# Attention scores over 64 rows throughout, a head's two maps in the two halves of the rows

## The chip, the core and the metric

The kernel runs on one core of one Trainium2 chip. The metric is the device time of one execution in microseconds; times are told as the median of several runs. Traces come from the hardware profiler, one execution each.

## The reference

One step of a hybrid decoder layer: 1024 prompt tokens and 8 single-token samples go through an input projection, four retention heads, four differential-attention heads, an output projection and a gated MLP. What the change touches is the differential attention over the prompt. Each of its four heads has two query and key maps of 64 features each:

```python
s = jnp.einsum('bqhmd,bkhmd->bhmqk', q, dk).astype(jnp.float32) * (DH_DIFF ** -0.5)
s = s + alibi_bias(qpos, kpos, slopes)[None, :, None]
a = diff_combine(jax.nn.softmax(s, axis=-1), lam)      # p[map 0] - lam * p[map 1]
return jnp.einsum('bhqk,bkhe->bqhe', a.astype(dv.dtype), dv)
```

`m` is the map (0 or 1), `d` runs over 64 features, the mask is causal, queries go in blocks of 128.

## The kernel before

**Precision.** Large products are made from values split in two float32r parts, hi and lo, as three matmuls: hi by hi, hi by lo, lo by hi.

**Phases.** Phase A makes the input projection in 28 blocks of 128 output features by three segments of 344 tokens; one block and segment is a "z unit" of 24 matmuls (lines 112 to 114). The stages of four attention heads (`diff_head`), then of four retention heads, and of the samples' paged attention are generators that are advanced between z units (lines 762 to 775), so that their matmuls stand among those of the projection. From about 570 us on come the output projection's norms, the MLP's two products and the end.

**Order.** The program is written with a framework that sets each engine's order ahead of time: instructions are taken in the order in which they were written, and when the next one's operand or buffer would not be there yet, later ones that are ready are put ahead of it. Each engine then works its list in that order and waits where data is late.

**One attention head.** A head's projected queries and keys lie in `zq` and `zk`, 128 rows by 1024 tokens: map 0 in rows 0 to 63, map 1 in rows 64 to 127. ScalarE and VectorE split them in hi and lo (lines 319 to 322). Then six copies from SBUF to SBUF, issued on SyncE's queue (lines 323 to 328), build doubled tiles for each map m: `qs[m]` holds the map's q_hi in one half of the rows and its q_lo in the other, `ks[m]` holds k_hi in both. So one matmul over 128 rows gives q_hi·k_hi + q_lo·k_hi, and a second one, over the 64 rows of map m, adds q_hi·k_lo (lines 342 and 343).

There are 8 stages per head, one for each block i of 128 queries; a stage has w = 128(i+1) keys. Each map's scores are made in one or two chunks of at most 512 keys, each chunk in a PSUM bank of the tag "S" (three banks). VectorE reads the bank, adds the bias and keeps the running minimum (line 345); ScalarE takes the exponential (397); VectorE combines the maps (406). Two stages later the result is transposed (`tr`) and multiplied with the values (`av_mm`, line 363). In a stage the order is: map 0 whole, map 1's first chunk, `av_mm(i-2)`, map 1's second chunk.

While a head is finished, the next one's copies wait in SyncE's queue together with the loads of weights (line 97) and cache pages (line 459).

Of the kernel before, what the change touches and what calls it, by code (L numbers as in the profile page):

```python
# [9 lines left out]
F32 = mybir.dt.float32  # L10
# [26 lines left out]
# columns of the constant block  # L37
# [14 lines left out]
def step_kernel(ctx: ExitStack, tc: tile.TileContext, gam, g128, xT, w_in, w_o, w_f, w_y, norms, ngb, cst, subln,  # L52
# [37 lines left out]
    # ---------------------------------------------------------------- helpers  # L90
# [26 lines left out]
    def rstd_1(pl, acc):  # L117
        """acc [128, n]: per-partition partial sums of squares -> diagonals of rsqrt(mean + eps), split."""
# [42 lines left out]
    # ================================================================ phase A  # L161
# [6 lines left out]
    # ---- load x, fold in the pre-norm gain, split  # L168
# [60 lines left out]
    # the first two blocks go segment by segment, as x comes in  # L229
# [27 lines left out]
    def tail_a():  # L257
# [6 lines left out]
        # lambda, sub-norm gain  # L264
# [32 lines left out]
    def sub_norm(on, n):  # L297
        """on [128, n, 128] *= rsqrt(mean over the last axis + eps), in place."""
# [9 lines left out]
    # ---- differential attention over the prompt, one head, in stages  # L308
    def diff_head(h):
# [3 lines left out]
        # scores: [q_hi; q_lo] against [k_hi; k_hi], then q_hi against k_lo  # L313
        lo_h, hi_h = slice(0, 64), slice(64, 128)
        ks = [pd.tile([P, 1024], F32R, name=f"ks{m}", tag=f"ks{m}") for m in range(2)]
        qs = [pd.tile([P, 1024], F32R, name=f"qs{m}", tag=f"qs{m}") for m in range(2)]
        kl = pd.tile([P, 1024], F32R, name="kl", tag="kl")
        ql = aux([P, 1024], name="ql", dt=F32R)
        nc.scalar.activation(qs[0], zq[:, 0:T], AF.Copy)
        nc.scalar.activation(ks[0], zk[:, 0:T], AF.Copy)  # L320
        nc.vector.tensor_tensor(ql, zq[:, 0:T], qs[0].bitcast(F32), ALU.subtract)
        nc.vector.tensor_tensor(kl, zk[:, 0:T], ks[0].bitcast(F32), ALU.subtract)
        nc.sync.dma_start(ks[1][lo_h].bitcast(F32), ks[0][hi_h].bitcast(F32))
        nc.sync.dma_start(ks[1][hi_h].bitcast(F32), ks[0][hi_h].bitcast(F32))
        nc.sync.dma_start(qs[1][hi_h].bitcast(F32), qs[0][hi_h].bitcast(F32))
        nc.sync.dma_start(qs[1][lo_h].bitcast(F32), ql[hi_h].bitcast(F32))
        nc.sync.dma_start(ks[0][hi_h].bitcast(F32), ks[0][lo_h].bitcast(F32))
        nc.sync.dma_start(qs[0][hi_h].bitcast(F32), ql[lo_h].bitcast(F32))
# [8 lines left out]
        def score(i, m, n0, w, pt, mn):  # L337
            r = slice(64 * m, 64 * m + 64)
            n1 = min(w, n0 + 512)
            sps = bank("S", "sps")[:, 0:n1 - n0]  # L340
            q = slice(i * P, (i + 1) * P)
            nc.tensor.matmul(sps, lhsT=qs[m][:, q], rhs=ks[m][:, n0:n1], start=True, stop=False)
            nc.tensor.matmul(sps, lhsT=qs[m][r, q], rhs=kl[r, n0:n1], start=False, stop=True)  # L343
            mo = pa.tile([P, 1], F32, tag="mn", bufs=6, name="mn")
            nc.vector.tensor_tensor_reduce(pt[:, n0:n1], sps, bias[:, 1024 - w + n0:1024 - w + n1],
                                           -1.0, mn, ALU.add, ALU.min, mo)
            return mo
# [32 lines left out]
        for i in range(8):  # L380
# [6 lines left out]
            pm_ = []  # L387
            for m in range(2):
                pt = aux([P, 1024], name="pt")
                mn = score(i, m, 0, w, pt, 3e38)  # L390
                if m == 1 and i > 1:
                    av_mm(i - 2)
                    if i == 5:
                        on0 = post1(0)
                if w > 512:
                    mn = score(i, m, 512, w, pt, mn)
                nc.scalar.activation(pt[:, 0:w], pt[:, 0:w], AF.Exp, bias=mn, scale=-1.0,
                                     accum_out=sm[:, m:m + 1])
                pm_.append(pt)
# [28 lines left out]
    # ---- paged differential attention of the samples, in stages of a page  # L428
    def sample_attention():
        ptt = pk.tile([1, NS * NPAGE], I32, name="ptt")  # L430
        nc.sync.dma_start(ptt, ptab)
        # queries as rows, one sample's row on every partition
# [101 lines left out]
        # weights with the keys on partitions: [key, page, sample, head]  # L534
# [64 lines left out]
    # ---- retention, one head, in stages  # L599
    def ret_head(h):  # L600
# [15 lines left out]
        # natural values and keys, and the decayed queries, take the places of the transposed ones  # L616
# [22 lines left out]
        # samples: the state's part, sample b in row 32 * (b % 4) + b // 4  # L639
# [11 lines left out]
        # the new key's part  # L651
# [6 lines left out]
        # new keys and values as rows, in three groups of 32: hi, lo, hi against hi, hi, lo  # L658
# [59 lines left out]
    # ---- the rest of the input projection, with the heads' stages woven in  # L718
# [70 lines left out]
    # what is left of the sides, beside the first output blocks' products with the finished heads  # L789
# [27 lines left out]
    split_last(2)  # L817
    closed(LATE["pk"], PR["cm"], LATE["pb"], pa_cm)

    # ================================================================ phase W: output projection, both norms  # L820
    wo_cm, wo = opened("wo")
    ft_cm, ft = opened("ft", "right")
    pw_cm, pw = opened("pw", "right")
# [429 lines left out]
```

## Time and profile before

| what | value |
|---|---|
| median of 3 runs | 1430.91 us |
| the runs | 1428.03, 1430.91, 1433.99 us |
| span of the profiled execution | 1426.5 us |
| TensorE matmul busy (PE) | 1382.5 us, 97% |
| VectorE busy (DVE) | 814.3 us, 57% |
| ScalarE busy (ACT) | 512.1 us, 36% |
| GpSimd busy (POOL) | 321.8 us, 23% |
| mean granted TensorE clock | 0.989 |

The profiled execution has no time on record beside its span; the median of the runs lies 4.4 us above the span, for what lies around the first and the last instruction. PE's matmuls are pipelined, so their durations overlap, and what one costs is read from start to start.

### The profile page before, as it was taken

How to read it: one execution, taken by the hardware profiler on the slowest of the kernel's cores; microseconds unless marked ns; L12 is line 12 of the kernel's file. 1: busy time of each engine (PE TensorE's matmuls, PEld its weight loads, DVE VectorE, ACT ScalarE, POOL GpSimd, SP SyncE). 2: the span in 40 equal slices, each digit the busy share in tenths (PEclk: the TensorE clock that was granted, in tenths of full speed). 3: DMA queues.
4: the chain of work that ended last, by engine and by line, in shares of the span. 5: the costliest groups of instructions: out<-in, count | busy, mean ns of one | idle time of the engine just before them, and what ended most of it. 6: DMA issues, size and time to landing. Idle time of an engine off the chain costs nothing.

```text
span 1426.5 us, 22325 instructions
## 1 busy us (share of the span) xinstructions
PE 1382.5 (97%) x8475; PEld 1315.5 (92%) x8475; DVE 814.3 (57%) x1656; ACT 512.1 (36%) x1016; POOL 321.8 (23%) x289
## 2 busy tenths in 40 slices
PE   6999989999999999999999999999999999989998
PEld 6979788888999999999999999999999999989976
DVE  7664677887589866477533323333232445575585
ACT  6243433426221225344322222222221235445544
POOL 4200084754355621332000000000000000050140
PEclk9999999999999999999999999999999999999999
DMA  5414166673355534132111101011110144344363
GB/s 214 120 48 118 41 191 198 218 212 118 132 175 177 165 129 150 60 140 110 68 52 37 60 31 60 33 57 45 45 60 30 60 169 145 121 156 141 119 201 124
DMA packets 67148, 161.59 MB, mean 113 GB/s; under 512 B 8283, under 2 KB 20699, under 8 KB 66659
## 3 DMA queue, kind: packets, MB, share of 16 engines
q1 hardware_dynamic: 60322, 148.57, 31.7%
q10 hardware_dynamic: 6720, 11.62, 2.2%
q8 instruction: 66, 1.08, 0.3%
q14 instruction: 40, 0.32, 0.1%
HBM read 134.93 MB, written 18.94 MB: 108 GB/s over the span
## 4 chain that ended last, share of the span: by engine, by line
PE 78%; DVE 9%; POOL 4%; issue 3%; DMA 3%; ACT 1%; SPq 0%; POOLq 0%; DVEq 0%; ACTq 0%
PE gp L112 6%; PE gp L113 6%; PE gp L114 6%; PE up L114 6%; PE up L113 6%; PE up L112 6%; PE ps_in L112 5%; PE ps_in L114 5%; PE ps_in L113 5%; PE ps_y L1063 4%; PE ps_y L1064 4%; PE ps_y L1062 4%; PE sps L343 2%; DVE acc_v L583 2%; PE ops L363 2%
## 5 line engine op out<-in xcount | busy, mean ns | idle before, releaser
L112 PE MATMUL ps_in<-xh,wh 128*128 128x344 f32 x672 | 227.0, 338 | 6.8 <-ACT xh L191 5.8
L113 PE MATMUL ps_in<-xl,wh 128*128 128x344 f32 x672 | 220.6, 328 | 2.3 <-DVE xl L192 2.3
L114 PE MATMUL ps_in<-xh,wl 128*128 128x344 f32 x672 | 221.2, 329 | 1.1 <-DVE wl L107 1.1
L112 PE MATMUL gp<-hh,wh 128*128 128x346 f32 x528 | 170.3, 322 | 0.0
L113 PE MATMUL gp<-hl,wh 128*128 128x346 f32 x528 | 170.0, 322 | 0.0
L114 PE MATMUL gp<-hh,wl 128*128 128x346 f32 x528 | 169.4, 321 | 0.0
L114 PE MATMUL up<-hh,wl 128*128 128x344 f32 x528 | 169.3, 321 | 0.0
L113 PE MATMUL up<-hl,wh 128*128 128x344 f32 x528 | 169.1, 320 | 0.0
L112 PE MATMUL up<-hh,wh 128*128 128x344 f32 x528 | 169.0, 320 | 0.0
L107 DVE TENSOR_TENSOR wl<-wraw,wh 128x1024 fp32r<-128x1024 f32 (+1 forms) x81 | 102.1, 1262 | 95.2 <-ACT wh L106 92.8
L106 ACT ACTIVATE wh<-wraw 128x1024 fp32r<-128x1024 f32 (+1 forms) x81 | 84.6, 1045 | 184.3 <-PE gp L113 92.0
L112 PEld LDWEIGHTS ps_in<-xh,wh 128*128 128x128 f32 x672 | 130.7, 194 | 12.8 <-ACT xh L191 5.8
L113 PEld LDWEIGHTS ps_in<-xl,wh 128*128 128x128 f32 x672 | 130.9, 195 | 4.1 <-DVE xl L192 3.7
L1013 DVE TENSOR_TENSOR wyl<-wyraw,wyh 128x1024 fp32r<-128x1024 f32 x66 | 83.5, 1265 | 87.8 <-ACT wyh L1012 86.5
L114 PEld LDWEIGHTS ps_in<-xh,wl 128*128 128x128 f32 x672 | 130.6, 194 | 2.0 <-DVE wl L107 1.4
L1062 PE MATMUL ps_y<-ah,wyh 128*128 128x388 f32 x352 | 120.4, 343 | 3.1 <-ACT wyh L1012 3.1
L1064 PE MATMUL ps_y<-ah,wyl 128*128 128x388 f32 x352 | 120.6, 343 | 0.2 <-DVE wyl L1013 0.2
L1063 PE MATMUL ps_y<-al,wyh 128*128 128x388 f32 x352 | 120.4, 342 | 0.4 <-DVE al L1024 0.4
L927 DVE SCALAR_TENSOR_TENSOR c<-gp,cwt,c 128x344 f32<-128x344 f32 (+1 forms) x66 | 37.7, 570 | 131.2 <-ACT c L925 131.2
L159 POOL TENSOR_TENSOR acc<-acc,sq 128x344 f32<-128x344 f32 (+1 forms) x56 | 58.4, 1043 | 226.4 <-ACT sq L158 160.6
L954 POOL COPY sct<-sct 128x176 f32<-128x176 f32 x1 | 0.5, 516 | 463.5 <-DVE sc L949 463.5
L925 ACT ACTIVATE c<-gp,cbt,cwt 128x344 f32<-128x344 f32 (+1 forms) x66 | 41.7, 632 | 175.3 <-PE gp L114 175.3
(251 smaller groups left out, 3008.5 us busy)
## 6 DMA issues: line engine op xcount, KB each, us to landing
wyraw<-in_w_y SPq DMA_DIRECT2D x66, 512.0 KB, 3.3
wraw<-in_w_f SPq DMA_DIRECT2D x44, 512.0 KB, 3.2
pg<-in_kpool SPq DMA_DIRECT2D x64, 256.0 KB, 3.1
pg<-in_vpool SPq DMA_DIRECT2D x64, 256.0 KB, 3.0
wraw<-in_w_in SPq DMA_DIRECT2D x27, 512.0 KB, 4.0
x<-in_xT SPq DMA_DIRECT2D x3, 1376.0 KB, 5.7
x1d<-x ACTq DMA_DIRECT2D x3, 1376.0 KB, 5.7
wraw<-in_w_o SPq DMA_DIRECT2D x8, 512.0 KB, 3.2
```

Source lines behind the costliest of these rows:

```text
L106: nc.scalar.activation(hi[:, k], raw[:, k], AF.Copy)
L107: nc.vector.tensor_tensor(lo[:, k], raw[:, k], hi[:, k].bitcast(F32), ALU.subtract)
L112: nc.tensor.matmul(ps, lhsT=wh[:, k, :], rhs=ah[:, k, n0:n1], start=(first and i == 0), stop=False)
L113: nc.tensor.matmul(ps, lhsT=wh[:, k, :], rhs=al[:, k, n0:n1], start=False, stop=False)
L114: nc.tensor.matmul(ps, lhsT=wl[:, k, :], rhs=ah[:, k, n0:n1], start=False, stop=(last and i == len(order) - 1))
L159: eng.tensor_tensor(acc, acc, sq, ALU.add)
L925: nc.scalar.activation(c[:, 0:n], gp[:, 2:2 + n], AF.Identity, bias=cbt[:, j:j + 1], scale=cwt[:, j, 2:3])
L927: nc.vector.scalar_tensor_tensor(c[:, 0:n], gp[:, 1:1 + n], cwt[:, j, 1:2], c[:, 0:n], ALU.mult, ALU.add)
L1013: nc.vector.tensor_tensor(wl, raw, wh.bitcast(F32), ALU.subtract)
L1062: nc.tensor.matmul(pss[d], lhsT=wh[:, i, w], rhs=ah, start=(f == 0), stop=False)
L1063: nc.tensor.matmul(pss[d], lhsT=wh[:, i, w], rhs=al, start=False, stop=False)
L1064: nc.tensor.matmul(pss[d], lhsT=wl[:, i, w], rhs=ah, start=False, stop=(f == NF - 1))
```

## The change

The doubled tiles and the six copies per head go. The four split tiles `qh`, `ql`, `kh`, `kl` keep both maps side by side in the two halves of the rows. `score` now makes both maps' chunk in one call: it takes two banks, and issues six matmuls over 64 rows, the two maps in turn (rows 0 to 63, then 64 to 127) for each of the three products. A stage's order is: both maps' first chunk, `av_mm(i-2)`, both maps' second chunk, then both exponentials. `ql` moves from the shared "aux" buffers to the pool `pd`. Elsewhere only comments are dropped.

```diff
-        ks = [pd.tile([P, 1024], F32R, name=f"ks{m}", tag=f"ks{m}") for m in range(2)]
-        qs = [pd.tile([P, 1024], F32R, name=f"qs{m}", tag=f"qs{m}") for m in range(2)]
-        kl = pd.tile([P, 1024], F32R, name="kl", tag="kl")
-        ql = aux([P, 1024], name="ql", dt=F32R)
-        nc.scalar.activation(qs[0], zq[:, 0:T], AF.Copy)
-        nc.scalar.activation(ks[0], zk[:, 0:T], AF.Copy)
-        nc.vector.tensor_tensor(ql, zq[:, 0:T], qs[0].bitcast(F32), ALU.subtract)
-        nc.vector.tensor_tensor(kl, zk[:, 0:T], ks[0].bitcast(F32), ALU.subtract)
-        nc.sync.dma_start(ks[1][lo_h].bitcast(F32), ks[0][hi_h].bitcast(F32))
-        nc.sync.dma_start(ks[1][hi_h].bitcast(F32), ks[0][hi_h].bitcast(F32))
-        nc.sync.dma_start(qs[1][hi_h].bitcast(F32), qs[0][hi_h].bitcast(F32))
-        nc.sync.dma_start(qs[1][lo_h].bitcast(F32), ql[hi_h].bitcast(F32))
-        nc.sync.dma_start(ks[0][hi_h].bitcast(F32), ks[0][lo_h].bitcast(F32))
-        nc.sync.dma_start(qs[0][hi_h].bitcast(F32), ql[lo_h].bitcast(F32))
+        kh, kl, qh, ql = (pd.tile([P, 1024], F32R, name=n, tag=n) for n in ("kh", "kl", "qh", "ql"))
+        nc.scalar.activation(qh, zq[:, 0:T], AF.Copy)
+        nc.scalar.activation(kh, zk[:, 0:T], AF.Copy)
+        nc.vector.tensor_tensor(ql, zq[:, 0:T], qh.bitcast(F32), ALU.subtract)
+        nc.vector.tensor_tensor(kl, zk[:, 0:T], kh.bitcast(F32), ALU.subtract)
...
-        def score(i, m, n0, w, pt, mn):
-            r = slice(64 * m, 64 * m + 64)
+        def score(i, n0, w, pts, mns):
             n1 = min(w, n0 + 512)
-            sps = bank("S", "sps")[:, 0:n1 - n0]
+            sps = [bank("S", "sps")[:, 0:n1 - n0] for _ in range(2)]
             q = slice(i * P, (i + 1) * P)
-            nc.tensor.matmul(sps, lhsT=qs[m][:, q], rhs=ks[m][:, n0:n1], start=True, stop=False)
-            nc.tensor.matmul(sps, lhsT=qs[m][r, q], rhs=kl[r, n0:n1], start=False, stop=True)
-            mo = pa.tile([P, 1], F32, tag="mn", bufs=6, name="mn")
-            nc.vector.tensor_tensor_reduce(pt[:, n0:n1], sps, bias[:, 1024 - w + n0:1024 - w + n1],
-                                           -1.0, mn, ALU.add, ALU.min, mo)
-            return mo
+            for j, (a, b) in enumerate(((qh, kh), (ql, kh), (qh, kl))):
+                for m in range(2):
+                    r = slice(64 * m, 64 * m + 64)
+                    nc.tensor.matmul(sps[m], lhsT=a[r, q], rhs=b[r, n0:n1], start=(j == 0), stop=(j == 2))
+            out = []
+            for m in range(2):
+                mo = pa.tile([P, 1], F32, tag="mn", bufs=6, name="mn")
+                nc.vector.tensor_tensor_reduce(pts[m][:, n0:n1], sps[m], bias[:, 1024 - w + n0:1024 - w + n1],
+                                               -1.0, mns[m], ALU.add, ALU.min, mo)
+                out.append(mo)
+            return out
...
-            pm_ = []
+            pm_ = [aux([P, 1024], name="pt") for _ in range(2)]
+            mns = score(i, 0, w, pm_, (3e38, 3e38))
+            if i > 1:
+                av_mm(i - 2)
+                if i == 5:
+                    on0 = post1(0)
+            if w > 512:
+                mns = score(i, 512, w, pm_, mns)
             for m in range(2):
-                pt = aux([P, 1024], name="pt")
-                mn = score(i, m, 0, w, pt, 3e38)
-                if m == 1 and i > 1:
-                    av_mm(i - 2)
-                    if i == 5:
-                        on0 = post1(0)
-                if w > 512:
-                    mn = score(i, m, 512, w, pt, mn)
-                nc.scalar.activation(pt[:, 0:w], pt[:, 0:w], AF.Exp, bias=mn, scale=-1.0,
+                nc.scalar.activation(pm_[m][:, 0:w], pm_[m][:, 0:w], AF.Exp, bias=mns[m], scale=-1.0,
                                      accum_out=sm[:, m:m + 1])
-                pm_.append(pt)
```

## Rows read from the trace of the kernel before

**Rows 1.** The page: its span, and busy time of the engines in all.

```profile
span 1426.5 us, 22325 instructions
...
PE 1382.5 (97%) x8475; PEld 1315.5 (92%) x8475; DVE 814.3 (57%) x1656; ACT 512.1 (36%) x1016; POOL 321.8 (23%) x289
```

**Rows 2.** Stretches: busy us (instructions) of PE, PEld, DVE, ACT, POOL; clock; DMA.

```profile
60.00:180.00 120.00, 119.92 (x679) 100.38 (x677) 67.24 (x191) 51.92 (x123) 5.01 (x10) 0.99 0.29 85
180.00:375.00 195.00, 186.53 (x1115) 164.34 (x1115) 156.19 (x341) 76.78 (x171) 118.97 (x95) 0.98 0.60 184
220.00:240.00 20.00, 19.99 (x95) 16.09 (x96) 15.84 (x48) 8.24 (x23) 12.80 (x11) 0.91 0.62 199
340.00:360.00 20.00, 19.56 (x110) 15.68 (x109) 20.00 (x45) 8.14 (x14) 14.12 (x12) 1.00 0.55 171
```

**Rows 3.** Line 342: count, min/median/max ns, first and last start, counts by shape.

```profile
L342 PE MATMUL sps<-ks,qs x96: 219/444/512, 75.2 to 356.1; 128*128 128x512 f32 x48, 128*128 128x128 f32 x16, 128*128 128x256 f32 x16, 128*128 128x384 f32 x16
```

**Rows 4.** PE in order of time, 112.8 to 115.4 us: start, duration, line.

```profile
112.78 1.60 PE L363 MATMUL ops<-z,pt 128*128 128x128 f32 x12
114.14 0.47 PE L342 MATMUL sps<-ks,qs 128*128 128x512 f32 x1
114.54 0.49 PE L343 MATMUL sps<-kl,qs 64*128 64x512 f32 x1
114.97 0.42 PE L112 MATMUL ps_in<-xh,wh 128*128 128x344 f32 x1
115.23 0.32 PE L113 MATMUL ps_in<-xl,wh 128*128 128x344 f32 x1
115.39 0.32 PE L114 MATMUL ps_in<-xh,wl 128*128 128x344 f32 x1
```

**Rows 5.** Weight loads (PEld) of the same stretch; in brackets idle time before.

```profile
114.54 0.18 PEld L343 LDWEIGHTS sps<-kl,qs 64*128 64x128 f32 x1 [0.24 <-issue]
114.96 0.19 PEld L112 LDWEIGHTS ps_in<-xh,wh 128*128 128x128 f32 x1 [0.24 <-issue]
115.07 0.19 PEld L113 LDWEIGHTS ps_in<-xl,wh 128*128 128x128 f32 x1
```

**Rows 6.** PE in order of time, 75.9 to 78.2 us, head 0's first scores.

```profile
75.91 0.32 PE L343 MATMUL sps<-kl,qs 64*128 64x128 f32 x1
76.16 0.38 PE L342 MATMUL sps<-ks,qs 128*128 128x256 f32 x1
76.48 0.38 PE L343 MATMUL sps<-kl,qs 64*128 64x256 f32 x1
76.79 0.38 PE L342 MATMUL sps<-ks,qs 128*128 128x256 f32 x1
...
77.41 0.45 PE L342 MATMUL sps<-ks,qs 128*128 128x384 f32 x1
77.78 0.44 PE L343 MATMUL sps<-kl,qs 64*128 64x384 f32 x1
78.15 0.46 PE L114 MATMUL ps_in<-xh,wl 128*128 128x344 f32 x1
```

**Rows 7.** PE in order of time at 1353 us, all matmuls of 128 rows.

```profile
1352.77 0.39 PE L1102 MATMUL ps_n<-wyh,ah 128*128 128x512 f32 x1
1353.00 0.39 PE L1103 MATMUL ps_n<-wyl,ah 128*128 128x512 f32 x1
```

**Rows 8.** PE in order of time at 430.6 us, 128 rows by 32 columns.

```profile
430.63 0.66 PE L558 MATMUL os_ps<-acc_v,ez 128*32 128x128 f32 x16
431.22 0.43 PE L112 MATMUL ps_in<-xh,wh 128*128 128x344 f32 x1
```

**Rows 9.** Instructions on the score banks: VectorE's pass over them.

```profile
L345 DVE CUSTOM_DVE_ANT_0 pt<-sps,bias x64: 280/682/693, 75.8 to 357.3; 128x512 f32<-128x512 f32 x40, 128x128 f32<-128x128 f32 x8, 128x256 f32<-128x256 f32 x8, 128x384 f32<-128x384 f32 x8
```

**Rows 10.** The chain that ended last, in order of time: start, us, what.

```profile
216.55 3.32 DMA ks<-ks
```

**Rows 11.** Waits from 60 to 380 us: waiter, releaser, total us, times, longest.

```profile
PE sps L342 <- DMA ks<-ks: 0.7, 1, 0.7
```

More of the change, by code (lines that the diff above doesn't have):

```diff
@@ L312, in diff_head @@
         nc.sync.dma_start(bias, alibi[h])
-        lo_h, hi_h = slice(0, 64), slice(64, 128)
-        ks = [pd.tile([P, 1024], F32R, name=f"ks{m}", tag=f"ks{m}") for m in range(2)]
-        qs = [pd.tile([P, 1024], F32R, name=f"qs{m}", tag=f"qs{m}") for m in range(2)]
-        kl = pd.tile([P, 1024], F32R, name="kl", tag="kl")
-        ql = aux([P, 1024], name="ql", dt=F32R)
-        nc.scalar.activation(qs[0], zq[:, 0:T], AF.Copy)
-        nc.scalar.activation(ks[0], zk[:, 0:T], AF.Copy)
-        nc.vector.tensor_tensor(ql, zq[:, 0:T], qs[0].bitcast(F32), ALU.subtract)
-        nc.vector.tensor_tensor(kl, zk[:, 0:T], ks[0].bitcast(F32), ALU.subtract)
-        nc.sync.dma_start(ks[1][lo_h].bitcast(F32), ks[0][hi_h].bitcast(F32))
-        nc.sync.dma_start(ks[1][hi_h].bitcast(F32), ks[0][hi_h].bitcast(F32))
-        nc.sync.dma_start(qs[1][hi_h].bitcast(F32), qs[0][hi_h].bitcast(F32))
-        nc.sync.dma_start(qs[1][lo_h].bitcast(F32), ql[hi_h].bitcast(F32))
-        nc.sync.dma_start(ks[0][hi_h].bitcast(F32), ks[0][lo_h].bitcast(F32))
-        nc.sync.dma_start(qs[0][hi_h].bitcast(F32), ql[lo_h].bitcast(F32))
+        kh, kl, qh, ql = (pd.tile([P, 1024], F32R, name=n, tag=n) for n in ("kh", "kl", "qh", "ql"))
[3 more added lines that the diff above has]
+        nc.vector.tensor_tensor(kl, zk[:, 0:T], kh.bitcast(F32), ALU.subtract)
         vn = zv[:, 0:T].rearrange("p (a b) -> p a b", b=P)
```

## The prediction

> **What bounds the kernel now.** I read the page first: TensorE is busy nearly all of the 1426.5 us span, no other engine above 57% [rows 1]. The stretches come next, since the change touches only the attention heads. Heads 0 and 1 lie between 60 and 180 us: PE has next to no idle time there, VectorE is busy 56%. Heads 2 and 3 lie between 180 and 375 us, where the samples' cache pages run too: PE idles 8.5 us of 195, VectorE is busy 80% in the mean and all of 340 to 360 us [rows 2]. So a microsecond of TensorE time saved in heads 0 and 1 should reach the end; in heads 2 and 3 VectorE stands close behind.
>
> Then the order of time on PE, because durations overlap and hide what a matmul costs. Between matmuls of 128 rows, start to start is 0.16 us for 344 columns [rows 4] and 0.23 for 512 [rows 7]: columns at 2.4 GHz, the upper level (granted clock near 1.00 [rows 2]), plus about 0.02. Around the 64-row matmul of line 343 this breaks: from line 342 to 343 0.40 us for 512 columns, from 343 to the next matmul 0.43, and from that one 0.26 where 0.16 is usual [rows 4]. The weight loads say why: at the change of 128 to 64 rows, and back, the load stands idle 0.24 us, starts only when the matmul before is through, and can't run ahead, while the second load after the change again follows at 0.11 us [rows 5]. So going into 64 rows costs 0.40 - 0.23 = 0.17 us and coming out 0.43 - 0.23 = 0.20, 0.37 in all; the further 0.10 behind it is taken as equal before and after.
>
> The Trainium skill, "TensorEngine Tiling (Array Packing)", Key Properties, says that changing the tiling mode drains the engine, and that changing only the tile doesn't. The trace agrees with the first half (0.37 us a round trip, rows 4 and 5); no row shows the second.
>
> **The scores before.** Line 342 has 96 matmuls: 48 of 512 columns, 16 each of 128, 256 and 384 [rows 3]; line 343 has as many. That is 24 pairs of maps with 512 columns and 8 each of the other widths. Start to start a map's two matmuls cost 0.40 + 0.43 at 512 columns [rows 4], 0.37 + 0.37 at 384, 0.32 + 0.31 at 256, and 0.25 twice at 128 (from line 343's row) [rows 6]. A pair of maps thus costs 1.66, 1.48, 1.26, 1.00 us, in all 24 x 1.66 + 8 x 3.74 = 69.8 us.
>
> **The scores after.** A pair becomes six 64-row matmuls in one block: one way in and out (0.37 us) in place of two. What the six cost is not shown before, since no two 64-row matmuls are neighbours there. Three bounds:
> - *Halves overlap, free weight loads*: three steps of 0.23, 0.18, 0.13, 0.07 us (columns plus 0.02), with 0.37: 1.06, 0.91, 0.76, 0.58. Change: 24 x -0.60 + 8 x (-0.57 - 0.50 - 0.42) = -26.3 us.
> - *Halves overlap, but loads go one by one* at the 0.11 us spacing [rows 5]: a step is at least 0.22: 1.06, then 1.03 for all others. Change: -14.4 + 8 x (-0.45 - 0.23 + 0.03) = -19.6 us.
> - *Halves one after the other*: six times 0.23, 0.18, 0.13, 0.11, with 0.37: 1.75, 1.45, 1.15, 1.03. Change: 24 x 0.09 + 8 x (-0.03 - 0.11 + 0.03) = +1.3 us. The half more columns eat what the saved changes give.
>
> Nearest to this are 16 matmuls of 128 columns over four groups of 32 array columns, 0.59 us from their first start to the next shape's [rows 8]; one by one they would be 16 x 0.07 = 1.1 us at least. So parts of the array do work at once here, by columns; by rows is my inference. I take the middle one, -19.6.
>
> The Trainium skill, "TensorE: Matmul & The Clock Gate", Part 3, says that matmuls in different row groups run at once; by it alone the sum would be the first bound's. Its section on LDWEIGHTS says that load time goes with columns and not rows, which the rows bear out (0.18 against 0.19 us, rows 5), and that is the second's.
>
> **Order and banks.** A pair needs two of three banks, so a second pair waits for VectorE's pass over the first pair's map 0, 0.69 us at 512 columns [rows 9], which now begins only near the block's end. In a stage of i >= 4 the cover is `av_mm`, 6 to 12 instructions of 0.11 us (12 in 1.36 [rows 4]), 0.7 to 1.3 us: just enough. Where stages follow each other without a z unit, only a few transposes cover it. Where a bank is late, map 0's three matmuls go ahead of map 1's and nothing overlaps. I take 12 of 48 pairs so: they gain nothing, and -19.6 becomes -14.7.
>
> **VectorE behind it.** Its instructions are the same in number and size. Heads 2 and 3 hold half of the saving, 7 us; with VectorE at 80% to 100% I take half of that as lost in waits: -14.7 + 3.5 = -11.2. Lost to nothing or wholly, that is -14.7 or -7.4.
>
> **The copies.** 24 issues go from SyncE's queue, six per head, and with them the time from split to first score. PE stood waiting for a copy once, 0.7 us [rows 11], at head 2's start, where a copy of 3.32 us is on the chain that ended last [rows 10]; behind it the clock was at its lower level for part of 220 to 240 us: mean 0.91, 0.09 x 20 = 1.8 us lost [rows 2]. Loads of weights and pages (lines 97, 459) queued behind these copies; they come sooner. Elsewhere z units hide the copies. Together 0 to -2.5; I take -2. `ql`'s move and the later exponentials I cost at nothing: two stages lie between the exponential and the transposes; if that cover fails PE would wait about one more exponential.
>
> **Sum:** -11.2 - 2 = -13 us on the span, 1413.5 us; with the 4.4 us that the median lies above the span, **1418 us**, -0.9%.
>
> **The rivals.**
> - *The halves don't overlap, or VectorE takes the gain back.* For: no row shows two halves at work together, and VectorE is full in 340 to 360 us [rows 2]. Against: columns overlap [rows 8], and heads 0 and 1 have slack. Time: +1.3 - 2, 1430 us, no change. The Trainium skill, "TensorEngine Tiling (Array Packing)", PSUM Bottleneck, warns of this: faster tiles don't empty the banks faster.
> - *The blocks break up.* When a bank or a transpose comes mid-block, 128-row matmuls get in and each map is an excursion of three again: per map 3 steps + 0.37 = 1.06, 0.91, 0.76, 0.70 against 0.83, 0.74, 0.63, 0.50, in all 48 x 0.23 + 16 x (0.17 + 0.13 + 0.20) = +19 us; with the copies 1448 us. Against: in the shown stretches line 342 and 343 stand together, with nothing of lines 112 to 114 between a map's two [rows 4, 6].
> - *Each change of half drains like a change of mode* (slower). Every one of the six then costs like line 343: 6 x 0.43, 0.37, 0.32, 0.25 + 0.17 = 2.75, 2.39, 2.09, 1.67, in all 24 x 1.09 + 8 x (0.91 + 0.83 + 0.67) = +45 us: 1474 us. It decides for slower by 0.5% from about 0.033 us per change on: (7.2 + 2 - 1.3) / (48 x 5).
>
> **How the numbers follow.** What a measurement of this kernel can tell from no change is about 0.5%, 7.2 us. Forecast 0.55 (0.51 faster, 0.04 same); no overlap or gain taken back 0.26 (0.03, 0.21, 0.02); broken blocks 0.11 (0, 0.02, 0.09); drains 0.08 (slower). Faster 0.54, same 0.27, slower 0.19. The range reaches from the first bound's full gain with the copies, 1430.9 - 28.3 = 1403, to 1440, past the second case and to the lower part of broken blocks; left out are the drains, most of broken blocks and a little below. The forecast's own range is 1403 to 1424.
>
> **What would show it.** Right: rows 0 to 63 and 64 to 127 starting within hundredths of a us of each other; steps of about 0.23 us per two 512-column matmuls; 48 blocks, not 96, each with one idle load in and one out; PE's time on scores near 50 us; the gain there already at 180 us, with more waits on VectorE behind it; no wait on copies. Wrong: a start 0.23 us behind its neighbour's (no overlap), 0.43 (drains), or lines 112 to 114 within a block (broken up). A clock at its lower level in the blocks would also upset the sum.

## The result, and the profile after

The changed kernel took **1437.57 us** in the median (1432.11 to 1442.05, 13 runs), the kernel before 1428.44 us (1425.71 to 1434.11, 13 runs) on the same chip: ratio 1.0055, 95% interval [1.0039, 1.0071]. It is slower by 0.55%, 9 us at the medians, where 13 us of gain were forecast.

The page of the changed kernel, span and busy times, answers to [rows 1]:

```profile
span 1432.6 us, 22455 instructions
...
PE 1369.0 (96%) x8571; PEld 1311.9 (92%) x8571; DVE 816.6 (57%) x1656; ACT 509.8 (36%) x1016; POOL 321.7 (22%) x289
```

TensorE is busy 13.5 us less, with 96 matmuls more, while the span is 6.1 us longer: the work went down and the idle time went up. The order of time on PE shows what became of a pair of maps, first at 512 columns, then at 128 (columns: start, duration, engine, line, tile, shapes, count; two instructions in one row start within hundredths of a us of each other):

```profile
78.69 0.38 PE L291 MATMUL tp<-ct,pt 128*128 128x128 f32 x2
79.01 0.51 PE L334 MATMUL sps<-kh,qh 64*128 64x512 f32 x2
79.34 0.40 PE L334 MATMUL sps<-kh,ql 64*128 64x512 f32 x2
79.58 0.41 PE L334 MATMUL sps<-kl,qh 64*128 64x512 f32 x2
79.91 0.71 PE L357 MATMUL ops<-z,pt 128*128 128x128 f32 x4
...
86.44 0.33 PE L334 MATMUL sps<-kh,qh 64*128 64x128 f32 x2
86.60 0.28 PE L334 MATMUL sps<-kh,ql 64*128 64x128 f32 x2
86.71 0.27 PE L334 MATMUL sps<-kl,qh 64*128 64x128 f32 x2
86.92 0.66 PE L291 MATMUL tp<-ct,pt 128*128 128x128 f32 x4
```

The halves do work at once: 0.24 us from the second two matmuls to the third two at 512 columns, and 0.11 us at 128 columns, where the one-by-one loads of the middle bound would have made it 0.22. The weight loads of the two halves start together as well:

```profile
79.01 0.19 PEld L334 LDWEIGHTS sps<-kh,qh 64*128 64x128 f32 x2 [0.17 <-issue]
79.11 0.19 PEld L334 LDWEIGHTS sps<-kh,ql 64*128 64x128 f32 x2
79.35 0.20 PEld L334 LDWEIGHTS sps<-kl,qh 64*128 64x128 f32 x2
```

A 512-column pair takes 0.90 us from its first start to the next instruction's, not the 1.66 of before.

The stretches answer to [rows 2] (from, to, length; busy us and count of PE, PEld, DVE, ACT, POOL; clock; DMA share; GB/s):

```profile
60.00:180.00 120.00, 117.69 (x784) 103.61 (x783) 73.68 (x206) 54.45 (x129) 13.84 (x16) 1.00 0.20 67
180.00:375.00 195.00, 170.68 (x1056) 153.77 (x1056) 149.48 (x324) 70.23 (x156) 109.16 (x88) 0.93 0.51 159
```

Between 180 and 375 us TensorE stands idle 24.3 us instead of 8.5, and its mean granted clock is 0.93 instead of 0.98 (1.00 is the upper of its two levels, 2.4 GHz). What it waited for there (total, times, longest):

```profile
PE sps L334 <- DVE mn L338: 10.1, 6, 4.1
PE tp L291 <- DVE pt L398: 8.9, 3, 4.2
PE tp L291 <- DVE z L219: 3.8, 2, 3.4
```

These waits, 22.8 us of the 24.9 that the view lists, are behind VectorE: score passes, combines, evacuations of z units. The wait for a copy [rows 11] is gone.

**Where the time went.** Progress is measured by z units: 24 matmuls of lines 112 to 114 each, counted in order of time from the start, so that unit n is the same work in both kernels. "Before" and "changed" are us from the start of one unit to the start of the other; idle is PE's within them. The two profiled executions lie 6.1 us apart, the medians 9.1; the table divides the former.

| z units | holds | before (idle) | changed (idle) |
|---|---|---|---|
| to 27 | heads 0 and 1 | 197.1 | 189.7 |
| 27 to 57 | heads 2 and 3, cache pages | 197.9 (7.1) | 211.4 (21.8) |
| of these 30 to 36 | head 2's core | 48.4 | 61.1 |
| of these 48 to 54 | head 3's core | 40.3 | 47.1 |
| 57 to 87 | retention heads | 164.8 (2.7) | 165.8 (3.4) |

Start to start, score matmuls cost 69.2 us before (34.5 + 34.7 for the two pairs of heads) and 44.5 after (20.7 + 23.7). The instructions beside them, transposes and `av_mm`, became dearer by 11 us in all; part of the way into and out of the 64-row blocks is now read there. Heads 0 and 1 bring 7.4 us, units 27 to 30 another 4.7 (3.2 of it idle time); head 2's core loses 12.7 and head 3's 6.8.

**Head 2's loss.** The chain of work that ended last, cut to 180 to 280 us, has this share by line in the changed kernel:

```profile
by line: DMA pg<-in_kpool 21.1%; DVE sc L473 11.7%; DVE pt L398 9.8%; POOL pg L482 9.6%; issue 7.3%; DVE wl L107 4.9%; DVE pt L338 4.9%; PE ps_in L114 4.0%; DVE z L219 3.7%; PE ps_in L112 3.5%; PE ps_in L113 3.4%; DMA wraw<-in_w_in 3.2%; DV
```

42.4% of it is the samples' key pages: load, GpSimd's product (482), VectorE's sum (473), which frees the buffer for the next load. The z units' matmuls have 10.9%. One turn of it, just behind unit 36 (start, duration, what), then VectorE and PE in order of time at the same place:

```profile
263.44 5.81 DMA pg<-in_kpool
...
269.38 1.30 POOL pg L482
...
270.71 0.69 DVE sc L473
...
272.98 2.28 DVE pt L398
```

```profile
270.71 0.69 DVE L473 TENSOR_REDUCE sc<-pg 128x8 f32<-128x512 f32 x1 [2.90 <-POOL pg L482]
271.31 0.14 DVE L395 COPY r<-rs 128x1 f32<-128x1 f32 x1
271.37 0.55 DVE L397 SCALAR_TENSOR_TENSOR cf<-sm,nlam,rs 128x1 f32<-128x1 f32 x1
271.84 1.21 DVE L317 TENSOR_TENSOR ql<-z,qh 128x1024 fp32r<-128x1024 f32 x1
272.98 2.28 DVE L398 SCALAR_TENSOR_TENSOR pt<-pt,cf 128x1024 f32<-128x1024 f32 x1
```

```profile
270.87 0.31 PE L114 MATMUL ps_in<-xh,wl 128*128 128x344 f32 x1
275.41 0.87 PE L291 MATMUL tp<-ct,pt 128*128 128x128 f32 x3 [4.22 <-DVE pt L398]
```

VectorE works its list in order. The sum's place comes, the page's product isn't there, VectorE stands 2.90 us; the combine behind it, which the transposes need, comes that much later, and PE stands 4.22 us. The split `ql` of the next head (1.21 us) stands between the two as well.

VectorE has more to do in head 2's core than before. Units 30 to 36 of the kernel before, then of the changed one:

```profile
214.90:263.30 48.40, 47.69 (x251) 38.85 (x249) 39.63 (x100) 20.25 (x50) 27.59 (x24) 0.96 0.63 206
202.70:263.90 61.20, 51.74 (x297) 43.72 (x295) 55.04 (x119) 19.77 (x51) 45.14 (x36) 0.89 0.63 189
```

It is busy 55.0 us of 61.2 where it was busy 39.6 of 48.4: 30 key sums (20.2 us) fall there in place of 17 (11.3 us), and its instructions take 9.8 us longer, in all, than the same ones in the kernels without page arithmetic (experiment 3), where it was 5.1. Since a longer stretch also takes in more page work, this alone doesn't say which came first.

### The profile page after: what moved, and what is told of

Same layout as the page of the kernel before. It is cut to its first block, busy times and chain, and to the rows that moved or that the text cites. A ratio compares the mean times of both kernels' runs of the same rounds, so it can differ in the third digit from the quotient of the medians.

```text
span 1432.6 us, 22455 instructions
## 1 busy us (share of the span) xinstructions
PE 1369.0 (96%) x8571; PEld 1311.9 (92%) x8571; DVE 816.6 (57%) x1656; ACT 509.8 (36%) x1016; POOL 321.7 (22%) x289
## 4 chain that ended last, share of the span: by engine, by line
PE 64%; DVE 11%; DMA 4%; POOL 4%; issue 3%; ACT 2%; SPq 0%; POOLq 0%; DVEq 0%; ACTq 0%
PE gp L112 6%; PE gp L113 6%; PE up L114 6%; PE gp L114 6%; PE up L113 6%; PE up L112 6%; PE ps_y L1055 3%; PE ps_y L1056 3%; PE ps_y L1054 3%; PE ps_in L112 3%; PE ps_in L114 3%; PE ps_in L113 3%; DVE acc_v L575 2%; POOL pg L482 2%; DMA pg<-in_kpool 1%
```

## The experiments

Ratios are to the kernel before on the same chip. Letters in the expectations: theory A blames the changed order within a stage, B the pages' load on VectorE in heads 2 and 3, C the missing copies, P the places of the page sums in VectorE's list, D the meeting of a faster TensorE with VectorE and GpSimd where the pages run.

**1. The order alone.** The tiles, copies and matmuls of before, in the changed order of a stage:

```diff
+            for m in range(2):
+                nc.tensor.matmul(sps[m], lhsT=qs[m][:, q], rhs=ks[m][:, n0:n1], start=True, stop=False)
+                nc.tensor.matmul(sps[m], lhsT=qs[m][r, q], rhs=kl[r, n0:n1], start=False, stop=True)
```

> The kernel before with its doubled tiles and its 128-row matmuls, but in the changed order: a call makes both maps' chunk in two banks, both exponentials come last. PE's work on scores is as before (69.8 us). Theory A (the pair in two of three banks, and the later exponentials, make TensorE stand wherever VectorE is late): slower by 8 to 20 us, with 10 us or more of waits of the scores on line mn between 60 and 380 us (before: 1.3). Theory B (the order does no harm; a shorter score stage alone meets VectorE's load from the cache pages in heads 2 and 3): within 5 us of before, waits on mn under 4 us.

1431.43 us, ratio 1.0007 [0.9991, 1.0023]. The scores' waits on `mn`, matmuls' and weight loads' together as in the expectations, are 6.4 us (1.3 before), between the two theories. The order does no harm by itself that shows in the time: A alone falls.

**2. One map at a time.** 64-row matmuls without copies, in the old order, each map's three in a row:

```diff
             for j, (a, b) in enumerate(((qh, kh), (ql, kh), (qh, kl))):
-                for m in range(2):
-                    r = slice(64 * m, 64 * m + 64)
-                    nc.tensor.matmul(sps[m], lhsT=a[r, q], rhs=b[r, n0:n1], start=(j == 0), stop=(j == 2))
+                nc.tensor.matmul(sps, lhsT=a[r, q], rhs=b[r, n0:n1], start=(j == 0), stop=(j == 2))
```

> The changed kernel's tiles and 64-row matmuls without copies, but one map after the other, in the order and with the one bank per call of the kernel before, so that the halves never work together. From the sum, each map is then three steps and 0.37 us: +19 us of TensorE time, -2 for the copies. Theory A: waits on mn back near before (under 4 us), 1440 to 1450 us in all, and the time lost lies evenly over the four heads. Theory B: the same time, since TensorE is no faster than before and VectorE never in the way.

1443.93 us, 1.0087 [1.0061, 1.0114]. The time lies where it was expected, but not for the reason given. The scores cost 49.6 us, 5 more than interleaved and 20 fewer than before, because the maps overlap without being written in turns (71 score matmuls start within 0.05 us of the one before, 114 in the changed kernel):

```profile
242.50 0.39 PE L333 MATMUL sps<-kl,qh 64*128 64x512 f32 x1
242.51 0.50 PE L333 MATMUL sps<-kh,qh 64*128 64x512 f32 x2
```

Map 0's third product and map 1's first start 0.01 us apart. Whether the framework's order or the engine brought them together wasn't looked into. The loss isn't spread over the four heads either: unit 27 starts 7.5 us sooner than in the kernel before, units 27 to 57 take 19.9 us longer, and the scores' waits on `mn` are 34 us, not under 4. So with cheap scores in the old order the kernel is slow too: the loss goes with the cheap scores and not with the pairing.

**3. No page arithmetic.** GpSimd's products and VectorE's sums of all key pages, and the products and sums of the value pages but the first of each sample, are left out, in both kernels; the loads stay in the program.

```diff
-                nc.gpsimd.tensor_tensor(kp, kp, qb.rearrange("p (a b) -> p a b", b=P), ALU.mult)
-                if held:
-                    reduce_page(*held)
-                held = (kp, b, p)
...
+                    if p:
+                        pass
```

> The changed kernel without the arithmetic on the samples' cache pages (the products and sums of the key pages, and all but the first value pages; the loads stay): VectorE and GpSimd are relieved in heads 2 and 3 alone. To be read beside the kernel before with the same work left out. Theory A: the bank waits stay in part, as the order is the same in all heads, and heads 0 and 1 have few: changed minus before between -12 and 0 us. Theory B: the whole saving of TensorE time reaches the end, changed minus before -18 to -25 us.

> The kernel before without the arithmetic on the samples' cache pages, as in the run beside it. Both theories: 5 to 15 us faster than before, since its idle time of some 8 us between 180 and 300 us goes.

Changed 1393.76 us, 0.9738 [0.9704, 0.9772]; before 1414.75 us, 0.9888 [0.9853, 0.9922]. Without the pages' arithmetic the change is worth 21.0 us. In units 9 to 27 TensorE's time for scores, transposes and `av_mm` together falls by 9.7 us, in 27 to 57 by 9.8. With the arithmetic the kernel before takes 14 us longer and the changed one 44.

The loads stay, but not in their place. With no product that holds a buffer, the last of the 64 key loads is issued at 133 us in the changed kernel and at 166 in the one before (with the arithmetic at 288 and 312). So these runs, and those of experiment 4 without key products, take the key pages' loads out of heads 2 and 3 together with the arithmetic.

**4. Parts of the pages.** The key half alone left out, then VectorE's key sums alone (`reduce_page`) with GpSimd's products kept, each in both kernels.

```diff
-                if held:
-                    reduce_page(*held)
                 held = (kp, b, p)
```

> The changed kernel with the key pages' arithmetic left out (GpSimd's product and VectorE's sum of each of the 64 key pages; their loads and the value pages' work stay). Without any page arithmetic the change was worth -21.0 us, with all of it +8.3. Theory 'each half at its head' (key pages cost head 2 its gain, value pages cost head 3 its): against the before kernel with the same omission the change is worth about half, -10 to -15 us, and z units 30 to 36 take about 48 us as before. Rival 'key pages alone': -20 us or so. Rival 'value pages alone': 0 to +8 us.

> The kernel before with the same work left out: the other side of the comparison. The whole page arithmetic cost it 14 us; about half of that here, 1420 to 1424 us.

> The changed kernel with VectorE's sums of the key pages left out, GpSimd's products kept. Theory 'VectorE's list is too full': this is worth nearly all that leaving out the whole key half is worth. Rival 'GpSimd at work stretches VectorE's instructions': with the products still running the combines (line 398's) stay near 2 us instead of 1.15, and at most half of it comes back.

> The kernel before with the same sums left out: the other side of the comparison. By either theory within 3 us of the kernel before without the whole key half.

| left out | before | changed | change is worth | PE idle, units 27 to 57, before / changed |
|---|---|---|---|---|
| nothing | 1428.44 | 1437.57 | +9.1 | 7.1 / 21.8 |
| key sums | 1425.07 | 1429.63 | +4.6 | 5.1 / 21.0 |
| key sums and products | 1416.67 | 1407.93 | -8.7 | 1.2 / 6.5 |
| all page arithmetic | 1414.75 | 1393.76 | -21.0 | 1.1 / 0.5 |

Each half costs its part: key pages 17.8 us of the swing, value pages 12.3. Of the key half, the sums are the smaller part, 4.5 us, of medians whose intervals are 2 to 3 us wide to each side. As the whole cause "VectorE's list is too full" doesn't hold: the changed kernel without sums is 8 us faster, but in the traces it gains 5.3 us before unit 27, and in units 27 to 57 TensorE idles as before. The other 13.3 us go when the products go too, and with them the loads that they hold back into these heads. The stretch from 180 to 280 us in the changed kernel without sums, then without the key half:

```profile
180.00:280.00 100.00, 86.51 (x514) 77.15 (x514) 63.66 (x114) 31.42 (x79) 80.83 (x63) 0.90 0.66 213
180.00:280.00 100.00, 99.77 (x660) 91.40 (x661) 49.88 (x138) 37.75 (x93) 6.07 (x9) 1.00 0.22 77
```

VectorE is busy 63.7 us in the first and TensorE still stands; in the second GpSimd is nearly idle, the DMA's 213 GB/s are 77, and TensorE hardly stands. Two expectations were missed: -8.7 us is less than the -10 to -15 of "each half at its head", and the kernel before without sums is 8.4 us slower than without the key half, not within 3; products and loads cost it too.

With products and without sums, POOL, DVE and PE in order of time:

```profile
181.54 8.75 POOL L482 TENSOR_TENSOR pg<-pg,qb 128x512 f32<-128x512 f32 x7
190.22 1.02 POOL L305 TENSOR_TENSOR rrn<-ss,ct 128x4 f32<-128x4 f32 x1
```

```profile
191.28 1.74 DVE L306 TENSOR_TENSOR on<-on,rrn 128x512 f32<-128x512 f32 x1 [7.17 <-POOL rrn L305]
...
211.27 0.86 DVE L397 SCALAR_TENSOR_TENSOR cf<-sm,nlam,rs 128x1 f32<-128x1 f32 x1
212.17 1.34 DVE L398 SCALAR_TENSOR_TENSOR pt<-pt,cf 128x128 f32<-128x128 f32 x1
```

```profile
193.17 1.09 PE L291 MATMUL tp<-ct,on 128*128 128x128 f32 x4 [4.80 <-DVE on L306]
```

and the same VectorE instructions in the changed kernel without the key half:

```profile
184.60 0.69 DVE L306 TENSOR_TENSOR on<-on,rrn 128x512 f32<-128x512 f32 x1 [1.18 <-POOL rrn L305]
...
203.13 0.21 DVE L397 SCALAR_TENSOR_TENSOR cf<-sm,nlam,rs 128x1 f32<-128x1 f32 x1
203.37 0.35 DVE L398 SCALAR_TENSOR_TENSOR pt<-pt,cf 128x128 f32<-128x128 f32 x1
```

Two ways show in this kernel. A small power on GpSimd (`rrn`, 1.02 us) stands behind a run of products, VectorE waits 7.17 us for it instead of 1.18, and PE 4.80 behind that. And beside running products VectorE's `on`, `cf` and combine take 1.74, 0.86 and 1.34 us instead of 0.69, 0.21 and 0.35. How much of the idle time is the one and how much the other wasn't separated.

In the full changed kernel the first way is small: between 170 and 380 us VectorE waits for `rrn` 2.8 us in all, 1.1 at the longest, and no wait of TensorE is put down to `on`. There VectorE's waits for GpSimd are those for key products, 15.4 us, and they were 13.1 in the kernel before. The second way is no larger over the whole of heads 2 and 3: measured against the kernels without page arithmetic, VectorE's instructions of units 27 to 57 are 15.9 us longer in the changed kernel and 19.3 in the one before. What the change adds is that both fall more on head 2 (in units 30 to 36 VectorE waits 3.6 us for GpSimd instead of 1.0, and its instructions are 9.8 us longer instead of 5.1). That TensorE has less work of its own to cover them is the likely rest, and not shown by itself.

The chain of the changed kernel without the key half, 180 to 280 us, is TensorE's own again, and head 2's core takes 45.4 us:

```profile
by line: PE ps_in L112 23.7%; PE ps_in L114 22.9%; PE ps_in L113 22.4%; PE sps L334 10.6%; PE ops L357 10.6%; PE tp L291 6.9%; POOL zs L223 1.2%; DVE pt L338 0.9%; DVE z L219 0.5%; DVE vd L487 0.2%; issue 0.2%; DVE mn L338 0.0%
```

Head 3's core still takes 47.0 us there, and 37.2 when the value pages' arithmetic is left out too: that loss is the value pages'. With and without the key half, VectorE there has eleven value sums in a row ahead of the next score passes; without it:

```profile
320.31 6.71 DVE L570 SCALAR_TENSOR_TENSOR acc_v<-pg,at,acc_v 128x128 f32<-128x128 f32 x11
```

In the full changed kernel they stand at 349.88 us (6.73 us), and PE waits 4.09 us for a score bank up to 359.40.

**5. The copies put back** (six per head; two of them feed `kc`, which is read in place of `kh`; four go to a tile that nothing reads):

```diff
+            for d, s in ((kc, kh), (dz, qh), (dz, ql)):
+                for r in (slice(0, 64), slice(64, 128)):
+                    nc.sync.dma_start(d[r].bitcast(F32), s[r].bitcast(F32))
```

> The changed kernel with six copies of 64 rows per head put back on SyncE's queue: two of them carry k_hi to a second tile that the scores read, four go to a spare tile that nobody reads. Scores, order and results are as in the changed kernel. Theory C (without the copies the heads start sooner and VectorE's and GpSimd's page work falls in with the scores worse): near the kernel before or faster, 1420 to 1430 us, bank waits under half of the changed kernel's 23 us. Theory D (heads 2 and 3 are held by VectorE and GpSimd working on pages and scores at once, copies or not): 1435 to 1445 us, waits as in the changed kernel.

1432.49 us, 1.0028 [1.0012, 1.0043]: 4 us by the ratios and 5 by the medians faster than without them, little more than the intervals leave, and between the ranges of C and D. The scores' waits on `mn` are as in the changed kernel (25.3 us, 23.5 there), not under half. GpSimd waits 28.4 us for key pages in 160 to 330 us, as before the change (29.7), where the changed kernel waits 15.7; in units 30 to 36 products fill 34.9 us of 54.6, not 42.9 of 61.1 (before: 26.1 of 48.4). Half of the key loads are issued by 232 us, not by 220 (before: 247): copies in SyncE's queue hold the page loads back, and fewer products fall within head 2. That this is where the time comes from is inferred; no wait of TensorE for a copy shows, and that the spare tile takes one of the eight shared "aux" buffers wasn't tried by itself.

**6. The pages' pace**, from 3 key pages per z unit to 2.5 and 2, and to 2 in the kernel before:

```diff
-D_RATE, R_RATE, K_PACE, V_PACE = 1.42, 0.88, 3.0, 2.35
+D_RATE, R_RATE, K_PACE, V_PACE = 1.42, 0.88, 2.5, 2.35
```

> The changed kernel with the key pages advanced by 2.5 in place of 3.0 per z unit, all else equal. Theory D: less page work falls beside the scores of head 2, and some of the 30 us that pages cost the changed kernel come back: 1420 to 1432 us. Theory C: no change beyond 4 us (1434 to 1441).

> The changed kernel with the key pages advanced by 2.0 in place of 3.0 per z unit. Theory D: more of the same, 1415 to 1428 us in spite of the later end of the value pages, which may leave some of the samples' work behind the heads. Theory C: 1434 us or more.

> The kernel before with the key pages advanced by 2.0 in place of 3.0 per z unit, as control for the run beside it. Theory D: pages cost the kernel before only about 14 us in all, so it gains less: 1420 to 1432 us, and the changed kernel at the same pace is faster than it by 5 us or more. Theory C: the changed kernel stays behind it.

1444.83 (1.0111 [1.0096, 1.0126]), 1458.68 (1.0205 [1.0191, 1.0220]) and 1456.25 us (1.0192 [1.0173, 1.0211]). All three miss theory D's ranges, and at pace 2 the changed kernel is not 5 us faster than the one before but 2 slower. But the pace didn't do in head 2 what the theory needs: GpSimd has begun 50 key products by unit 36 at each of the paces 3, 2.5 and 2, and head 2's core takes 61.1, 63.3 and 62.8 us. So D wasn't tested there. What the pace moved came later: at 2.5 unit 57 starts 8.0 us sooner than in the changed kernel, but the pages now end late, and unit 90 starts 11.5 us later.

**7. Page sums held** behind the latest z evacuation (key sums in both kernels; value sums too in the changed one):

```diff
+            with tc.issue_after(LASTZ["i"]):
+                nc.vector.tensor_reduce(sc[:, p, :, 2 * b:2 * b + 2], kp.rearrange("p h (m e) -> p h m e", m=2),
+                                        AX.X, ALU.add)
```

> The changed kernel, with each key page's sum on VectorE kept, in VectorE's list, behind the projection's evacuation (line 219) that was written last before it; nothing else is changed and no work is left out. In the changed kernel 49 of these sums stand before z unit 36 on VectorE, in the kernel before 37. Theory P (the framework's order puts some 12 page sums ahead, between the scores of head 2, and TensorE waits behind them): by unit 36 about 36 sums, units 30 to 36 last 48 to 52 us in place of 61, and the whole is 8 to 14 us faster than the changed kernel, 1423 to 1429 us. Theory D (too much work on VectorE and GpSimd in heads 2 and 3 whatever its order): within 4 us of the changed kernel, 1434 to 1441.

> As the run beside it, and VectorE's share of the value pages too is kept behind the evacuation written last before it. Theory P: head 3 (units 48 to 54, 47 us in the changed kernel against 40 before) gains too, 1418 to 1426 us. Theory D: within 4 us of the changed kernel.

> The kernel before with its key page sums held in the same way, as control. Theory P: its sums already stand at 37 by unit 36, so next to nothing changes, 1426 to 1432 us. If holding helps it as much as the changed kernel, the order of pages is no cause of the difference between the two.

1440.57 (1.0070 [1.0050, 1.0091]), 1440.05 (1.0074 [1.0048, 1.0100]) and 1432.62 us (1.0020 [1.0004, 1.0035]). With the key sums held, head 2's core takes 54.9 us; with the value sums held too, head 3's takes 40.5, as before the change. Yet by unit 90 the kernel with both held is only 0.5 us ahead of the changed one. Head 2's core then holds 22 sums, not 30, and is still over the 48 to 52 us that P wanted; what the second has gained by unit 57 (7.6 us) goes in units 57 to 87. Moved sums move the waits: P, that these orders would cure it, falls.

**8. Four score banks** (one for transposes):

```diff
-    NB = {"mm": 2, "S": 3, "t": 2, "o": 1}
+    NB = {"mm": 2, "S": 4, "t": 1, "o": 1}
```

> The changed kernel with four banks for scores in place of three, and one in place of two for transposes. Theory A (a pair in two of three banks is what TensorE waits for): waits of scores on mn fall from 23 us to under 8; if one bank for transposes costs nothing, 1420 to 1430 us. Theory P: waits move from the scores to other places, no gain, 1434 to 1445 us.

1432.21 us, 1.0018 [1.0003, 1.0033]. Scores cost 37.7 us (18.5 + 19.2). The scores' waits on `mn` fall from 23.5 to 4.2 us, as A said, but the time is still above A's range. In units 27 to 57 PE still idles 22.2 us, now for the most part behind ScalarE:

```profile
PE tp L291 <- ACT pt L348: 6.8, 2, 5.9
PE tp L291 <- ACT z L321: 4.9, 1, 4.9
PE tp L291 <- ACT mtd L368: 4.3, 2, 2.6
```

The fourth bank is worth 5 us, and 6.8 on the scores. It doesn't shorten TensorE's idle time as a whole.

**9. Sums two pages behind the products**, with a fifth page buffer, then with four score banks:

```diff
-PG_BUFS, AHEAD, TAIL = 4, 2, 2
+PG_BUFS, AHEAD, TAIL = 5, 2, 2
...
-                if held:
-                    reduce_page(*held)
-                held = (kp, b, p)
+                if len(held) == 2:
+                    reduce_page(*held.pop(0))
+                held.append((kp, b, p))
```

> The changed kernel with VectorE's sum of a key page written two pages behind GpSimd's product instead of one, and a fifth page buffer so that as many pages are loaded ahead as before. Theory 'VectorE's list waits for GpSimd' (in the changed kernel VectorE stood 15.4 us before key sums whose product was not there yet, with z evacuations, combines and score passes queued behind): that wait falls below 6 us, PE's waits on line 338, 398 and 219 fall by about as much, and 5 to 10 us come back: 1428 to 1433. Rival 'GpSimd's pace and the stretching of VectorE's instructions beside it, wherever the sums stand': the wait moves or falls, the time stays within 3 us of the changed kernel's 1437.6.

> The same with a fourth score bank (one bank fewer for transposes), which alone gave 1432.2. If the two causes add, 1422 to 1428, at or below the kernel before; if they are the same stall seen twice, 1430 to 1434.

1437.95 us, 1.0056 [1.0034, 1.0077], and 1435.93 us, 1.0054 [1.0034, 1.0074], the second above both of its ranges: the fourth bank's 5 us don't add. VectorE's wait for products fell only from 15.4 to 11.2 us (170 to 380 us), not below 6, and PE's idle time in units 27 to 57 from 21.8 to 20.1. So the first didn't take the wait away and can't clear the sums' wait of its share. No version that does the whole work beat the kernel before.

## Why the prediction was wrong

**Right.** The scores' cost before: 69.8 us summed, 69.2 read. The halves overlap; a bank that is late breaks that up (of 144 times possible, a score matmul starts within 0.05 us of the one before it 114 times, and 143 with four banks); there is no wait on copies; the gain of heads 0 and 1 is there (unit 27, at 190 us, starts 7.4 us sooner, unit 30 12.2). The term for late banks, 4.9 us, was near: a fourth bank saves 6.8 us of scores. Of the 4.4 us from span to median about half is what lies around the first and last instruction (1434.65 us against a span of 1432.6 in the changed kernel's profiled execution); the rest is that executions differ.

**Right by the wrong terms.** The middle bound was taken for loads that go one by one. They don't (two per 0.11 us), so the first bound holds: without page arithmetic the scores fell by 27.6 us (its sum: 26.3). But transposes and `av_mm` beside the blocks rose by 8.1, a term that the sum didn't have, and 19.5 us are left (9.7 + 9.8), late banks included, where the sum had 14.7. PE's time on scores was 44.5 us, not 50. That matmuls in different row groups run at once, the rule of the Trainium skill's "TensorE: Matmul & The Clock Gate", Part 3, by which the sum would have been the first bound's, is borne out (0.24 us per two).

**The step that failed: "VectorE behind it".** Half of heads 2 and 3's saving was taken as lost, 3.5 us, and the whole of it, -7.4, as the worst. Measured, units 27 to 57 lost it all and 13.5 us more, and PE's idle time there rose by 14.7. Three things were missed in it. GpSimd was not in the step at all, though the stretches had it busy 61% there [rows 2]; 13.3 us of the key half's 17.8 come with its products and the loads that go with them. The loss was bounded by the gain, as if a TensorE that is ahead could at worst wait until the old time; but the pages' own course moved too (unit 36 starts at 264 us, before at 263, and finds 50 products begun, not 39), and with them VectorE's work in head 2's core grew, from 39.6 to 55.0 us busy. And the mean granted clock was lower, 0.89 in 180 to 280 us against 0.97, and the z units' matmuls of units 27 to 57 took 2.8 us longer.

The row that could have shown it is the chain of waits cut to the stretch. For the kernel before, 180 to 280 us, it reads:

```profile
by line: DMA pg<-in_kpool 13.1%; POOL pg L490 12.5%; PE sps L343 7.8%; PE ps_in L112 7.6%; issue 7.2%; DVE sc L481 6.9%; PE ps_in L114 6.7%; PE ps_in L113 6.7%; DVE pt L406 5.8%; PE sps L342 5.8%; PE ops L363 3.9%; DMA ks<-ks 3.3%; DVE wl L
```

Pages had 32.5% of that chain, and the scores 13.6%, while PE was busy 93.2 us of the 100. Of the chain only its one copy was used [rows 10].

**"The copies": -2 us.** The sign was wrong: put back, they made the changed kernel 4 to 5 us faster. "Loads of pages come sooner" was right, and was counted as good; it brought more of GpSimd's products into head 2 (31 begin in units 30 to 36, 26 with the copies).

**The rivals.** Nearest came "VectorE takes the gain back", at 1430 us, but with the halves overlapping, with GpSimd as the main part, and by 30 us (from -21.0 to +9.1) where it had 12. Drains at each half did not occur. Blocks broke only in part: the 288 matmuls stand in 53 unbroken runs, 35 of them of one whole pair, where the rival had 96 of one map.

**Open.** How the 13.3 us divide between VectorE's waits for GpSimd, its instructions stretched beside it, and the loads that leave with the products; a test would move the products off GpSimd, or keep the loads in their place without products, and neither was tried. Also why products crowd more in head 2 in all kernels with cheap scores than in the kernel before: with the copies back 8 of the 16.8 us of difference go (42.9, 34.9 and 26.1), the rest was not traced. Over the eleven kernels with cheap scores and products, units 30 to 36 take 61 to 64 us in the four where products fill 43 of them and sums run too, 59.8 in the one without sums, where they fill 44, and 53 to 55 in the six where they fill 32 to 40. That the two go together is no proof; as causes only leaving the products out (45.4 us) and putting the copies back were tried.

## What to carry to other kernels

Read the chain of waits for the stretch that an edit touches, not only the busy shares: here TensorE was busy 93% of a stretch whose chain was one third a loop of other engines, and time saved on it turned into waits. Don't bound such a loss by the gain: sooner work, and loads that come sooner, crowd into in-order lists elsewhere. Leaving the neighbour's work out of both kernels (here -21 us without pages, +9 with) tells in two runs whether a saving is real and whose work eats it; look in the trace what else moved, as the loads did here.

## What the runs showed of the hardware

Matmuls over rows 0 to 63 and 64 to 127 ran at once with their weight loads, two 512-column ones in 0.24 us and two 128-column ones in 0.11, and did so even where only the end of one map met the start of the other (0.01 us apart). VectorE's slowing beside GpSimd's products depended on the instruction. The combine of 128 columns went from 0.35 to 1.34 us and `cf`, of one column, from 0.21 to 0.86; in the same stretch the score pass of 128 columns, which reads PSUM, took 0.29 us in both kernels, and the reciprocal of two columns 0.16:

```profile
209.41 0.29 DVE L338 CUSTOM_DVE_ANT_0 pt<-sps,bias 128x128 f32<-128x128 f32 x1
...
211.01 0.16 DVE L394 RECIPROCAL rs<-sm 128x2 f32<-128x2 f32 x1
...
218.73 0.21 DVE L397 SCALAR_TENSOR_TENSOR cf<-sm,nlam,rs 128x1 f32<-128x1 f32 x1
218.98 0.62 DVE L398 SCALAR_TENSOR_TENSOR pt<-pt,cf 128x384 f32<-128x384 f32 x1
```

These are of the changed kernel without key sums; the last two rows fall between two products (one ended at 218.02 us, the next began at 220.60), and both instructions are back at the times that they have without the key half, 0.21 and 0.62. The DMA engines were busy 86% of the time between these products, so here it's the products and not the loads that slow VectorE:

```profile
218.00:220.60 2.60, 2.60 (x19) 2.01 (x18) 1.49 (x5) 1.59 (x4) 0.01 (x1) 1.00 0.86 303
```
